# A hand-written planner gets new prices: TensorE's durations, a port that VectorE and GpSimd share, and the time at which an attention head's inputs land

## The chip, the cores and the metric

One core of one Trainium2 chip. The metric is the device time of one launch in microseconds (us), lower is better. Engines: TensorE (PE; its weight loads are listed as PEld), VectorE (DVE), ScalarE (ACT), GpSimd (POOL) and SyncE (SP), which here issues nearly all DMAs.

## The reference

One layer of a hybrid encoder, for two request groups that share the weights: 16 meta tokens and 512 prompt rows, and 64 new rows of a running stream, so 592 rows of 2048 columns, all fp32.

```
h = rms_norm(x, pre_gain)
g_q, g_k, g_v, g_z, g_r, s_q, s_k, s_v, s_z, m_gla, m_sb = split(h @ w_in)      # 2048 x 11280
o_gla = gated linear attention(g_q, g_k, g_v, decay from g_r)                  # 4 heads, 128 x 256 state
o_sb  = stick-breaking attention(s_q, s_k, s_v)                                # 8 heads, 1024 past keys for the 64 rows
y_gla = (rms_norm(o_gla) * silu(g_z)) @ w_up_gla;  y_sb = (o_sb * silu(s_z)) @ w_up_sb
y = x + rms_norm((sigmoid(m_gla) * y_gla + sigmoid(m_sb) * y_sb) @ w_o, post_gain)
```

Also returned are the new keys, the new values and the final states of the linear attention.

## The kernel before, in words

The four large products (`w_in`, `w_up_gla`, `w_up_sb`, `w_o`) are made on TensorE in three passes: each fp32 operand is split into a high part and a remainder (names ending in `h`/`hi` and `l`/`lo`), and high x high, high x low and low x high are added up in PSUM. The products with `w_in` and all but the first pair of `w_o` use a seven-product Strassen form on 2x2 blocks. The work is cut into *units* of 12 matmuls of 128x128 weights by 288 (or 296) columns. For each unit ScalarE rounds the weights (`convert`, tile `whi`), VectorE forms the remainder (`remain`, tile `wlo`), and at most four units are converted ahead of TensorE. The Strassen sums of weights (`combine`, `raw<-raw`) and the sums of results (`queue`: tiles `u`, `out`) run on VectorE; in one pair of columns the last product, S4 (reads block `h2`), may start only when the product S2 has been taken out of its bank by VectorE's `u` additions. A pair has the products W11, W22, S3, S1, S2, W12, S4, which read the blocks h0, h6, h5, h3, h4, h1, h2.

The attention runs in the background of these units, as generators: `decays` and four `gla_head`s one after the other (with `gla_side`, which takes half of a head's levels), then the eight heads of the stick-breaking attention, each as five chains (`sb_chain`, two of them interleaved). After the last unit of `w_in` come the two up-projections, then `w_o` and the final norm.

The order of the instructions on every engine is fixed when the program is built. A `Plan` keeps for each engine the time at which it is free and for each tile the time at which it is ready, and prices every instruction with `cost`. `Plan.run` holds one stream for each of the generators (`convert`, `remain`, `combine`, `multiply`, `queue`, ..., the background); again and again it takes the stream whose `due` time is the earliest, lets it issue its next instructions, and `note` moves the times on:

```
def due(self, e):
    return max(e["ready"] + e["slack"], self.free.get(e["eng"], 0.0)) - self.lead.get(e["name"], 0.0)
```

`e["ready"]` of a stream is `plan.last` at its last yield; `note` sets `plan.last` to the end of each priced instruction. In `w_in` the leads are 0.4 for `remain` and `combine`, 0 for `queue`, -0.1 for `multiply`; background streams have a slack of 0.4. So the prices decide nothing but the order in which instructions stand on the engines. On the chip every engine goes through its own list in that order and waits where an operand is not there.

The change touches `Plan.__init__`, a new `Plan.shared`, `Plan.cost`, `Plan.note`, and the start of `gla_head`. There a head takes `st["at"]`, the planned landing of its inputs k, cs and q (`gla_fetch`: five DMAs on SP and three small memsets on POOL), a tile `sc` is cleared by POOL, the flag ("load", hh) lets `gla_side` begin (its first instructions are VectorE's `x<-cs` subtractions), and `gla_diag` issues TensorE's products `b<-q,k`. The inputs of head 0 are fetched when the head begins; those of heads 1 to 3 while the head before is being normed, if g_q and g_k are stored by then.

Of the kernel before, what the change touches and what calls it, by code (L numbers as in the profile page):

```python
# [9 lines left out]
F32 = mybir.dt.float32  # L10
# [68 lines left out]
class Plan:  # L79


    def __init__(self):
        self.free, self.ready, self.used, self.last, self.streams = {}, {}, {}, 0.0, []
        self.base, self.now = {}, 0.0
        self.quartered, self.psum, self.lead, self.by = set(), set(), {}, {}

    def names(self, x):
# [8 lines left out]
    def at(self, x):  # L96
        return max(self.ready.get(y, 0.0) for y in self.names(x))

    def cost(self, eng, name, out, ins, summed):
        n = 1  # L100
        for x in out.shape[1:]:
            n *= x
        psum = any(x.tensor.name in self.psum for x in ins)
        if eng == "pe":
            dt = ins[0].dtype
            if dt == BF16:
                return 0.107
            if name == "transpose":
                return 0.053 if n < 64 else 0.11
            return max(0.214, n * 1.67e-3) if dt == F32 else max(0.11, n * 0.42e-3) + 0.003  # L110
        if eng == "act":
            return (0.055 if psum else 0.095) + (0.09 if summed or len(ins) > 1 else 0.0) + n * 0.83e-3
        if eng == "dve":
            if name == "tensor_scalar" and not psum:
                return 0.07 + n * 0.52e-3
            return 0.07 + n * (6.3e-3 if name == "reciprocal" else 1.04e-3)
        if name == "memset":
            return 0.04 + n * 0.83e-3
        return 0.15 + n * (3.5e-3 if name == "tensor_scalar" else 2.1e-3)

    def note(self, eng, name, args, kw):
        aps = [x for x in list(args) + list(kw.values()) if isinstance(x, bass.AP)]
        out = kw["out"] if "out" in kw else args[0]
        ins = [x for x in aps if x is not out]
        names = [y for x in ins for y in self.names(x)]
        outs = self.names(out)
        made = outs[1:] or outs
        if "dma" in name:
            size = 4.0
            for x in out.shape:  # L130
                size *= x
            start = max([self.now, self.free.get(eng, 0.0)] + [self.ready.get(x, 0.0) for x in names] + [self.base.get(outs[0], 0.0)])
            self.free[eng] = start + 0.5
            self.free["dma"] = max(self.free.get("dma", 0.0), start + 1.9) + size / 350e3
            end = self.free["dma"] + 1.8
            for x in made:
                self.ready[x] = max(self.ready.get(x, 0.0), end)
            for x in names:
                self.used[x] = max(self.used.get(x, 0.0), end)
            return  # L140
        start = self.free.get(eng, 0.0)
        for x in names + outs:
            by = self.by.get(x)
            if eng != "pe" or by != "pe":
                start = max(start, self.ready.get(x, 0.0) + LATENCY.get((by, eng), 0.1))
        end = start + self.cost(eng, name, out, ins, "accum_out" in kw)
        self.free[eng] = end
        for x in names + outs:
            self.used[x] = max(self.used.get(x, 0.0), end)
        for x in made:  # L150
            self.ready[x] = self.base[x] = end
            self.by[x] = eng
        self.last = end
# [54 lines left out]
def hybrid_step_kernel(ctx: ExitStack, tc: tile.TileContext, a, o):  # L208
    nc = tc.nc
    plan = Plan()  # L210
    sync, act, dve, pool, pe = (
        Engine(plan, key, e)
        for key, e in (("sp", nc.sync), ("act", nc.scalar), ("dve", nc.vector), ("pool", nc.gpsimd), ("pe", nc.tensor))
    )
# [513 lines left out]
    st = Region("st", "right")  # L728
# [480 lines left out]
    def gla_head(hh):  # L1209
# [3 lines left out]
            gla_fetch(hh)  # L1213
        st = gst[hh]
        k, cs, q = st["k"], st["cs"], st["q"]
        plan.last = max(plan.last, st["at"])
        sc = st["sc"] = r.tile([P, GC], F32, "sc")
        pool.memset(sc, 0.0)
        yield
        gdone.add(("load", hh))  # L1220
        yield from gla_diag(hh)
# [13 lines left out]
        end = r.tile([P, 6], F32, "end")  # L1235
# [5 lines left out]
        t = plan.last  # L1241
# [6 lines left out]
        t = plan.last  # L1248
        tokens(v0, scratch["gv", 2 * hh])
        at = plan.last  # L1250
# [10 lines left out]
        for j in range(2):  # L1261
            s = r.tile([P, 5, P], F32, "s")
            s5 = r.tile([P, P], F32, "s5")
            t = plan.last
# [41 lines left out]
            t = plan.last  # L1306
# [8 lines left out]
        t = plan.last  # L1315
# [3 lines left out]
        at = plan.last  # L1319
# [27 lines left out]
        for j in range(2):  # L1347
            yield "dve"
            x = o_t[j][:, :TO]
            dve.scalar_tensor_tensor(x, x, ggain[:, hh, j : j + 1], rs, op0=ALU.mult, op1=ALU.mult)  # L1350
        plan.last = max(plan.last, at)
        for j in range(2):
            yield "dve"
            x = o_t[j][:, :TO]
# [367 lines left out]
    def background():  # L1722
# [10 lines left out]
        for hh in range(GH):  # L1733
            yield from gla_head(hh)
# [239 lines left out]
```

## Time and profile before

| | |
|---|---|
| time, median of 3 runs | 1744.12 us (1739.87 to 1744.42) |
| time of the profiled execution | 1741.68 us |
| its span, first to last instruction | 1739.9 us |
| TensorE busy | 1670.2 us, 96% of the span |
| VectorE busy | 1250.6 us, 72% |
| ScalarE busy | 853.8 us, 49% |
| GpSimd busy | 182.2 us, 10% |
| mean granted TensorE clock | 0.986 of full speed |

The profiled execution lies inside the three runs, and 1.8 us of its time lie outside the span. All engine instructions go through one helper, so they carry the line L197, and groups are told apart by the names of their tiles: `wlo<-raw,whi` is the remainder, `b` is a PSUM bank. Consecutive instructions of one engine overlap a little in the trace (the end of one lies behind the start of the next), so a run of n instructions in a row tells the price of one better than the duration of a single one.

### The profile page before, as it was taken

Reading aid. Unit: us, or ns where it says so; the run is one execution under the profiler, and the core shown is the slowest. Engines: PE = TensorE matmul, PEld = TensorE weight load, DVE = VectorE, ACT = ScalarE, POOL = GpSimd, SP = SyncE. Lnnn points to the kernel's source line nnn. Section 1 sums busy time; section 2 is a strip of 40 time slices with the busy share of each in tenths; the row PEclk is TensorE's granted clock in tenths of the full one; section 3 lists DMA queues with packets and bytes.
Section 4 is the critical chain, followed back from the end, with each engine's and each line's share of the span. In section 5 each row is a group of like instructions: output and inputs, shape, how many; then the busy total and the mean of one; then the engine's idle time right before and its main releaser. Section 6 shows DMA issues by size and latency. Waiting matters only on the chain.

```text
span 1739.9 us, 31534 instructions
## 1 busy us (share of the span) xinstructions
PE 1670.2 (96%) x12089; PEld 1610.1 (93%) x12089; DVE 1250.6 (72%) x2081; ACT 853.8 (49%) x1759; POOL 182.2 (10%) x293
## 2 busy tenths in 40 slices
PE   4998999899999999999999999999999999999997
PEld 2798999889999998999999999999999999999996
DVE  5877878887987886886677667666766435687777
ACT  5554444344454353455565555555544323355554
POOL 2100220120130021021020011111000000000000
PEclk9999999999999999999999999999999999999998
DMA  7144234344444424455445544554447444423336
GB/s 189 37 140 131 77 107 139 101 116 123 122 117 128 132 60 119 126 163 159 133 137 152 148 140 117 158 158 126 128 138 218 143 142 124 122 79 103 104 80 218
DMA packets 323904, 224.14 MB, mean 129 GB/s; under 512 B 17436, under 2 KB 293432, under 8 KB 322584
## 3 DMA queue, kind: packets, MB, share of 16 engines
q1 hardware_dynamic: 323016, 219.49, 44.3%
q10 hardware_dynamic: 736, 2.62, 0.4%
q8 instruction: 95, 1.56, 0.4%
q14 instruction: 57, 0.47, 0.1%
HBM read 179.17 MB, written 42.90 MB: 128 GB/s over the span
## 4 chain that ended last, share of the span: by engine, by line
PE 89%; DVE 5%; DMA 2%; ACT 1%; issue 1%; POOL 1%; SPq 0%; DVEq 0%; ACTq 0%; POOLq 0%
PE b L197 89%; DVE wlo L197 2%; DVE raw L197 1%; DMA xt<-in_x_sample 1%; ACT whi L197 0%; DVE u L197 0%; DVE t L197 0%; DMA q<-d_gq 0%; POOL h5l L197 0%; DMA xt<-in_x_prompt 0%; DVE x L197 0%; POOL L L197 0%; DVE out L197 0%; SPq L197 0%; DMA raw<-in_w_in 0%
## 5 line engine op out<-in xcount | busy, mean ns | idle before, releaser
L197 ACT CAST whi<-raw 128x512 fp32r<-128x512 f32 x786 | 482.0, 620 | 627.6 <-PE b L197 516.2
L197 DVE TENSOR_TENSOR wlo<-raw,whi 128x512 fp32r<-128x512 f32 x786 | 552.6, 713 | 303.9 <-ACT whi L197 293.7
L197 DVE TENSOR_TENSOR raw<-raw 128x1024 f32<-128x1024 f32 (+1 forms) x232 | 259.5, 1121 | 6.0
L197 PE MATMUL b<-m,whi 128*128 128x288 f32 x912 | 183.5, 296 | 0.0
L197 PEld LDWEIGHTS b<-m,whi 128*128 128x128 f32 x912 | 146.1, 188 | 0.0
L197 PE MATMUL b<-h0h,whi 128*128 128x288 f32 (+1 forms) x480 | 134.3, 304 | 1.3 <-ACT whi L197 1.3
L197 PE MATMUL b<-m,wlo 128*128 128x288 f32 x456 | 134.2, 294 | 0.0
L197 PE MATMUL b<-h6h,whi 128*128 128x288 f32 (+1 forms) x480 | 133.8, 303 | 0.0
L197 PE MATMUL b<-h6l,whi 128*128 128x288 f32 (+1 forms) x480 | 131.5, 298 | 1.9 <-DVE h6l L197 1.8
L197 PE MATMUL b<-h4h,whi 128*128 128x288 f32 (+1 forms) x480 | 133.0, 302 | 0.0
L197 PE MATMUL b<-h1h,whi 128*128 128x288 f32 (+1 forms) x480 | 132.1, 300 | 0.0
L197 PE MATMUL b<-h0l,whi 128*128 128x288 f32 (+1 forms) x480 | 131.5, 299 | 0.0
L197 PE MATMUL b<-h4l,whi 128*128 128x288 f32 (+1 forms) x480 | 130.4, 296 | 0.0
L197 PE MATMUL b<-h1l,whi 128*128 128x288 f32 (+1 forms) x480 | 130.3, 296 | 0.0
L197 PE MATMUL b<-h0h,wlo 128*128 128x288 f32 (+1 forms) x416 | 124.4, 299 | 1.5 <-DVE wlo L197 1.5
L197 PE MATMUL b<-h4h,wlo 128*128 128x288 f32 (+1 forms) x416 | 123.2, 296 | 1.6 <-DVE wlo L197 1.6
L197 PE MATMUL b<-h1h,wlo 128*128 128x288 f32 (+1 forms) x416 | 123.3, 296 | 0.8 <-DVE wlo L197 0.8
L197 PE MATMUL b<-h6h,wlo 128*128 128x288 f32 (+1 forms) x416 | 123.7, 297 | 0.0
L197 PE MATMUL b<-h2h,whi 128*128 128x288 f32 (+1 forms) x352 | 112.5, 319 | 10.7 <-DVE u L197 10.7
L197 PE MATMUL b<-h2h,wlo 128*128 128x288 f32 (+1 forms) x352 | 107.5, 305 | 1.0 <-DVE wlo L197 1.0
L197 PE MATMUL b<-h5h,whi 128*128 128x288 f32 (+1 forms) x352 | 108.5, 308 | 0.0
L197 PE MATMUL b<-h3h,whi 128*128 128x288 f32 (+1 forms) x352 | 107.9, 307 | 0.0
(263 smaller groups left out, 4084.8 us busy)
## 6 DMA issues: line engine op xcount, KB each, us to landing
raw<-in_w_in SPq DMA_DIRECT2D x176, 512.0 KB, 4.5
raw<-in_w_o SPq DMA_DIRECT2D x32, 512.0 KB, 4.0
raw<-in_w_up_gla SPq DMA_DIRECT2D x16, 512.0 KB, 5.3
raw<-in_w_up_sb SPq DMA_DIRECT2D x16, 512.0 KB, 4.7
d_mg<-out SPq DMA_DIRECT2D x16, 288.0 KB, 2.2
d_ms<-out SPq DMA_DIRECT2D x16, 288.0 KB, 2.1
gate<-d_mg SPq DMA_DIRECT2D x16, 288.0 KB, 5.4
gate<-d_ms SPq DMA_DIRECT2D x16, 288.0 KB, 5.5
```

The costliest lines, as they stand in the source:

```text
L197: return real(*args, **kw)
```

## The change

Four edits to the planner and one to the start of a head; no instruction is added, removed or resized.

```diff
@@ Plan.__init__
+        self.port = {"pool": [], "dve": []}
...
+    def shared(self, out, ins):
+        n = [x for x in ins if x.tensor.name not in self.psum and x.shape[1:] == out.shape[1:]]
+        return len(n) > 1
@@ Plan.cost
             if dt == BF16:
-                return 0.107
+                return 0.056
             if name == "transpose":
-                return 0.053 if n < 64 else 0.11
-            return max(0.214, n * 1.67e-3) if dt == F32 else max(0.11, n * 0.42e-3) + 0.003
+                return 0.11
+            return max(0.224, n * 1.67e-3 + 4e-3) if dt == F32 else max(0.112, n * 0.4167e-3 + 0.0125)
...
+            if name == "scalar_tensor_tensor" and len(ins) > 2:
+                return 0.125 + n * 1.04e-3
@@ Plan.note
-        end = start + self.cost(eng, name, out, ins, "accum_out" in kw)
+        took = self.cost(eng, name, out, ins, "accum_out" in kw)
+        if name != "memset" and (eng == "pool" or eng == "dve" and self.shared(out, ins)):
+            for t0, t1 in sorted(self.port["pool" if eng == "dve" else "dve"]):
+                if t0 < start + took and t1 > start:
+                    start = t1
+            self.port[eng] = self.port[eng][-23:] + [(start, start + took)]
+        end = start + took
@@ gla_head
-        plan.last = max(plan.last, st["at"])
+        t = plan.last
         sc = st["sc"] = r.tile([P, GC], F32, "sc")
         pool.memset(sc, 0.0)
+        plan.last = max(t, st["at"])
         yield
```

- TensorE: a matmul of a unit (288 columns) goes from 0.1240 to 0.1325 us, one of 296 columns from 0.1273 to 0.1358; fp32 matmuls rise by 0.004 to 0.01 us, short transposes from 0.053 to 0.11, and bfloat16 ones fall from 0.107 to 0.056.
- VectorE: a `scalar_tensor_tensor` with three tensor inputs costs 0.055 us more.
- The port: a GpSimd instruction other than a memset, and a VectorE instruction with two inputs in SBUF, are moved behind every instruction of the other engine, among its last 24 of that kind, that they would overlap.
- The landing: `note` set `plan.last` to the end of the memset of `sc`, over the landing time taken just before; now the landing time is taken behind the memset, together with the stream's own time `t`.

## Rows read from the trace of the kernel before

**Rows 1.** The page, part 1: busy us (share of the span) xinstructions.

```profile
PE 1670.2 (96%) x12089; PEld 1610.1 (93%) x12089; DVE 1250.6 (72%) x2081; ACT 853.8 (49%) x1759; POOL 182.2 (10%) x293
```

**Rows 2.** Busy us (x instructions) by stage: PE, PEld, DVE, ACT, POOL, clock, DMA.

```profile
150.00:680.00 530.00, 500.69 (x3640) 489.94 (x3639) 429.49 (x712) 246.31 (x485) 88.82 (x113) 0.97 0.40 114
680.00:1266.00 586.00, 584.75 (x4267) 561.23 (x4266) 399.26 (x617) 320.28 (x632) 67.54 (x144) 1.00 0.49 139
1350.00:1700.00 350.00, 350.00 (x2639) 350.00 (x2639) 223.56 (x392) 150.66 (x338) 0.00 (x0) 1.00 0.39 110
```

**Rows 3.** PE's waits, 150 to 680 us: total, times, longest.

```profile
PE b L197 <- DVE u L197: 10.7, 3, 4.2
PE b L197 <- DVE cs L197: 5.8, 4, 2.7
PE b L197 <- DMA q<-d_gq: 5.5, 1, 5.5
PE b L197 <- DVE wlo L197: 3.4, 5, 1.6
PE b L197 <- DMA x<-d_gv: 2.7, 2, 1.4
PE b L197 <- DVE x L197: 1.3, 3, 0.6
```

**Rows 4.** PE's waits, 680 to 1700 us.

```profile
PE b L197 <- POOL L L197: 1.2, 3, 0.4
PE b L197 <- DVE h6l L197: 1.0, 1, 1.0
```

**Rows 5.** Busy us in the six stretches of halved clock, 150 to 680.

```profile
167.50:174.20 6.70, 3.55 (x16) 3.58 (x17) 2.72 (x6) 1.71 (x3) 1.19 (x1) 0.50 0.33 112
...
sum 33.30, PE 24.36 PEld 24.45 DVE 21.11 ACT 8.92 POOL 8.06; mean PE 4.06 PEld 4.08 DVE 3.52 ACT 1.49 POOL 1.34
```

**Rows 6.** Timeline of PE, 163 to 176: start, us, instruction, [idle before <-releaser].

```profile
164.81 0.29 PE L197 MATMUL b<-h2h,wlo 128*128 128x288 f32 x1
170.65 2.05 PE L197 MATMUL b<-q,k 128*128 128x128 f32 x8 [5.54 <-DMA q<-d_gq]
```

**Rows 7.** Timeline of SP and of DVE, 154 to 182.

```profile
165.42 0.84 SPq L197 DMA_DIRECT2D q<-d_gq  x2
...
164.87 2.48 DVE L197 TENSOR_TENSOR raw<-raw 128x1024 f32<-128x1024 f32 x2
169.97 0.90 DVE L197 TENSOR_TENSOR x<-cs 128x320 f32<-128x320 f32 x2 [2.62 <-DMA cs<-d_cs]
170.78 0.69 DVE L197 TENSOR_TENSOR wlo<-raw,whi 128x512 fp32r<-128x512 f32 x1
```

**Rows 8.** Timeline of DVE and of POOL, 362 to 380.

```profile
365.01 4.83 DVE L197 TENSOR_TENSOR wlo<-raw,whi 128x512 fp32r<-128x512 f32 x3 [0.27 <-ACT whi L197]
376.27 2.49 DVE L197 TENSOR_TENSOR wlo<-raw,whi 128x512 fp32r<-128x512 f32 x4
...
365.30 2.03 POOL L197 TENSOR_TENSOR x<-x,k 128x640 f32<-128x640 f32 x1
367.28 2.01 POOL L197 TENSOR_TENSOR q<-q,x 128x640 f32<-128x640 f32 x1
```

**Rows 9.** Timeline of DVE and of POOL, 300 to 322, where head 1 begins.

```profile
306.23 0.75 DVE L197 TENSOR_TENSOR x<-x,s 128x576 f32<-128x576 f32 x1
310.72 0.89 DVE L197 TENSOR_TENSOR x<-cs 128x320 f32<-128x320 f32 x2 [3.74 <-DMA d_og<-x]
...
317.00 2.48 DVE L197 TENSOR_TENSOR raw<-raw 128x1024 f32<-128x1024 f32 x2
319.40 0.95 DVE L197 TENSOR_TENSOR u<-u,b 128x296 f32<-128x296 f32 x2
...
303.87 0.63 POOL L197 MEMSET sc<- 128x640 f32 x1 [14.00 <-PE b L197]
```

**Rows 10.** DVE's waits, 150 to 680 us: total, times, longest.

```profile
DVE x L197 <- DMA d_og<-x: 7.4, 3, 3.7
```

## The prediction

> **What bounds the kernel now.** I read the page's busy shares first [rows 1]: TensorE is busy for 1670 of 1740 us, so the kernel is bound by TensorE, and no edit here removes a matmul. Only the time in which it stands still or runs slowly can be won. To see where that is I took the busy times by stage [rows 2]. From 1350 to 1700 us (up-projections and `w_o`) it is busy in all of the 350 us, and 2639 matmuls start in them, one every 0.1326 us. From 680 to 1266 us (stick-breaking attention) 1.3 us are missing. From 150 to 680 us (linear attention) 29.3 us are missing of 530, with VectorE busy in 81% of it. The waits of TensorE give the causes: in that stage `u`, `cs`, `wlo` and `x`, all made by VectorE (21.2 us together), then the inputs of a head (5.5) and of its values (2.7) [rows 3]; later, two small ones [rows 4]. The rest of its idle time is the start, before 75 us, and the last 24 us.
>
> Idle time is not all. The stage's granted clock is 0.97 [rows 2], and the stretches of low clock are six, each beside one of the longer waits: there the clock is 0.50, the lower of its two levels (1.2 of 2.4 GHz), and TensorE is busy for 24.4 of 33.3 us [rows 5]. Work at half speed loses half of its time, 12.2 us. So the whole stake in the stage is 29.4 + 12.2 = 41.6 us, 2.4% of the time.
>
> **The change part by part.** The edits change prices in the planner, so they act only through the order.
>
> *The landing.* TensorE finishes the first half of S4 at 165.10 and then stands for 5.54 us in front of `b<-q,k` of head 0, until q lands [rows 6]; the other half of S4, 12 matmuls, stands behind it in the list. VectorE waits 2.62 us in front of `x<-cs` in the same way [rows 7]. The planner put these there because the memset's end overwrote the landing time. After the change the stream of head 0 comes back only at the landing that the planner works out, 1.9 us + 0.97 MB at its 350 GB/s (2.8) + 1.8 = 6.5 us from the first issue, and up to 3 us more where weights are still under way. The trace has 170.65 - 165.42 = 5.2 us from the issue of q to its first reader [rows 6, 7], and four issues of some 0.4 ahead of it, 6.9: the planner is near enough, or late, which costs nothing while units are left. What moves is the whole start of the head: its diagonal products on TensorE, VectorE's two masked copies and the first `x<-cs` of both streams, ScalarE's exponentials and GpSimd's products. Its five DMAs stay where they are in SP's list; the stores behind them follow later or earlier with VectorE. Gain: 5.54 us of wait, and in the half-clock stretch right behind it 3.55 us of work that loses 1.78 [rows 5]: 7.3. What is late next: the next pair's first `wlo`. VectorE is at `raw<-raw` until 167.35, then needs 0.69 [rows 7], so `wlo` is there at 168.04, while TensorE ends S4 at 165.10 + 12 x 0.1326 = 166.69. Up to 1.35 us of a new wait remain. I take 6.6 (bounds 6.0 and 7.3).
>
> For heads 1 to 3 the inputs were fetched early, and the landing is past. But the stream's time changes too: it was the memset's end, 303.87 + 0.63 = 304.50 for head 1, and is now the end of the norm's last product, 306.98 [rows 9], 2.5 us later. There VectorE stands 3.74 us in front of `x<-cs`, because a store still reads the tile that it overwrites; the `wlo` and `raw` behind it are late, and the `u` that S4 needs comes at 319.40. A later start may let some of those pass. All three head changes have this wait, 7.4 us in sum [rows 10]. I count this edit inside the term of the two edits below.
>
> *TensorE's prices.* A unit was priced 12 x 0.1240 = 1.488 us, and is now 1.590; the trace has 12 x 0.1326 = 1.591 [rows 2]. The planner thought TensorE 6.5% faster against the other engines than it is, and so expected operands to be wanted earlier, and VectorE to be more behind, than is true. The fp32, transpose and bfloat16 prices and the `scalar_tensor_tensor` one concern background instructions alone. I put them at nothing: the units cover them, as the full stages show [rows 2]; without that cover they would be worth as much as the small waits, 1.2 us [rows 4].
>
> *The port.* Three `wlo` took 4.83 us while GpSimd ran two products of 2 us; four `wlo` without GpSimd took 2.49, 0.62 each [rows 8]. So VectorE stood 2.97 us for GpSimd's sake, and the planner did not know. Each head makes one such pair, before its `cs` copies, and `cs` is what TensorE waits for four times, 2.7 us at the longest [rows 3]. The edit does not remove the blocking; it lets the planner put what needs a late VectorE later on TensorE, with units ahead of it.
>
> The Trainium skill (SBUF — State Buffer, section Who interferes with whom) says that whichever of the two starts first holds the shared port for its whole instruction, and the other waits for that one instruction. Rows 8 agree. The planner goes further: it sends an instruction behind each recorded one that it would overlap until a gap of its own length comes, so by that rule it now believes GpSimd later than it is, and half of the next term's gain would go: 1735.
>
> What the two edits are worth: the stake left is 29.4 - 5.5 = 23.9 us of waits and 12.2 - 1.8 = 10.4 of clock, 34.3 together. The bounds are 0 and 34.3. The part after GpSimd's pairs (`cs` 5.8, `wlo` 3.4 [rows 3], and some 3 of clock, an estimate: a quarter of the 12.2) is 12 us; I take half of it, 6. Of the `u` waits, which hang on the store that no edit touches, and their clock, some 18 us, I take 1. That is 7.
>
> *What a new order costs.* The stages that are full now need not stay so. Bounds: 0, and 18 us (rival 3). I take 3, nearer the rows, which show 2.2 us of such waits in 1020 us [rows 4].
>
> Sum, against the profiled execution's own 1741.7 (2.4 under the median of the runs): 1741.7 - 6.6 - 7 + 3 = **1731**. Own range: 1724 to 1738.
>
> **The rivals.**
> 1. *The true prices clear most of the stage.* All waits but the store's and the values' are from a planner that did not know how late VectorE was. Then 60% of the 34.3 goes too: 1741.7 - 7.3 - 20.6 = 1714. For it: the waits are few and long (three of `u` make 10.7 us), each with a half-clock stretch behind it. Against: `remain` and `combine` keep their lead of 0.4 over `queue`, so a late VectorE still makes `wlo` and `raw` ahead of `u`, as happened where `u` came behind two `raw` [rows 9].
> 2. *It only shifts.* Head 0 starts later, VectorE's bunch of `raw`, `wlo` and `u` meets the first levels in another place, and another wait of 4 us with its clock takes the place of the one removed. The time stays at 1741. For it: VectorE has only 100 us left in the stage [rows 2].
> 3. *The cheap TensorE was a cushion* (slower). With units priced 6.5% short, TensorE came later to each background product than planned, and its operands were there. Stick-breaking attention has 8 heads x 5 chains x 3 such arrivals (scores, tails, values) = 120, of which 3 wait now, 1.2 us [rows 4]. With the true price, what else is priced short shows. If each of 120 waits 0.15 us, that is 18 us: 1741.7 - 6.6 + 18 = 1753. For it: nothing else in the planner covers such errors but the slack of 0.4. Against: TensorE is always behind there, so a product is placed behind a queue of units. It decides from 12 us of waits between 680 and 1266 on.
>
> **How the numbers follow.** Forecast 0.4, rival 1 0.2, rival 2 0.2, rival 3 0.2. A measurement of this kernel tells about 0.3% from no change, 5.2 us around 1744.1: under 1738.9 is faster, over 1749.3 slower. The forecast and rival 1 are faster, 0.6; rival 2 same, 0.2; rival 3 slower, 0.2. The range reaches just past the middle of rival 1's and to that of rival 3: 1712 to 1753.
>
> **What the profile after would show.** Right: no wait of TensorE on `q<-d_gq` over 1 us and no half-clock stretch near 167; `cs` waits under 3 us in sum; the stage's missing time near 18 us; 680 to 1700 still full. Wrong: `u` waits of more than 11 us in sum (rival 2), waits on `L`, `t` or `h` of many short pieces (rival 3), or a stage with under 8 us missing (rival 1). It would also be wrong if the last 24 us, whose order the new prices shuffle too and where every instruction is on the path, grew by more than 3 us.

## The result and the profile after

The change makes the kernel slower by half a per cent. Over six runs each on the same chip the median goes from 1741.83 us (1737.65 to 1744.42) to 1751.47 us (1749.03 to 1755.23); the ratio is 1.0056, with an interval of 1.0039 to 1.0074, outside the 0.3% that a measurement of this kernel can tell. The forecast of 1731 us had the wrong sign. The time lies outside the forecast's own range (1724 to 1738) and inside the wide one (1712 to 1753) only because that one was drawn out to rival 3's time. The profiled execution took 1752.33 us with a span of 1750.5.

The busy times by stage, in the columns of [rows 2], with one more line for the hand-over from `w_in` to the up-projections:

```profile
150.00:680.00 530.00, 502.54 (x3635) 489.63 (x3634) 430.08 (x704) 250.47 (x490) 86.12 (x111) 0.97 0.40 114
680.00:1266.00 586.00, 583.15 (x4261) 561.29 (x4261) 404.15 (x627) 315.86 (x628) 68.56 (x147) 1.00 0.50 140
1266.00:1350.00 84.00, 80.67 (x567) 78.34 (x566) 52.99 (x78) 39.12 (x63) 3.19 (x4) 0.96 0.57 169
1350.00:1700.00 350.00, 350.00 (x2639) 350.00 (x2638) 221.44 (x386) 149.71 (x337) 0.00 (x0) 1.00 0.40 114
```

The linear attention's stage has not been cleared. It misses 27.5 us of 530, where it missed 29.3 [rows 2], and its clock is still 0.97. TensorE's waits in it (150 to 680 us; total, times, longest) are others than before:

```profile
PE b L211 <- DVE x L211: 10.2, 5, 4.5
PE b L211 <- ACT whi L211: 5.2, 3, 2.1
PE b L211 <- DMA x<-d_gv: 4.6, 3, 3.4
PE b L211 <- DVE u L211: 3.8, 1, 3.8
PE b L211 <- DVE wlo L211: 2.4, 5, 0.7
...
PE b L211 <- DMA q<-d_gq: 0.2, 1, 0.2
```

Against [rows 3] the waits on `cs` (5.8) and `q` (5.5) are gone and those on `u` fall from 10.7 to 3.8; but `x`, the decayed queries and keys of the heads, grows from 1.3 to 10.2, `whi` comes in with 5.2 and the values grow from 2.7 to 4.6. Each wait of 2 us or more still lies beside a stretch of half clock. In place of the six stretches of [rows 5] there are five, and they are as long in sum (length, then the busy times):

```profile
sum 33.60, PE 24.73 PEld 23.66 DVE 27.84 ACT 12.73 POOL 8.62; mean PE 4.95 PEld 4.73 DVE 5.57 ACT 2.55 POOL 1.72
```

The timeline of TensorE shows the landing's repair and what follows it. The first product of head 0 stands 38 us later than in [rows 6] and waits 0.20 us instead of 5.54; the first long wait on a level product behind it is 4.45 us:

```profile
208.99 1.13 PE L211 MATMUL b<-q,k 128*128 128x128 f32 x8 [0.20 <-DMA q<-d_gq]
...
247.29 1.09 PE L211 MATMUL b<-x 128*128 128x64 f32 x4 [4.45 <-DVE x L211]
```

The later place is not the landing's doing. In e11 (below), which lacks the landing edit, the product starts at 208.6; in e4, which lacks the port edit, at 175.9.

A new loss lies at the hand-over. The last block of the linear attention's result is loaded (`stage`), and ScalarE waits for it before it makes `h6l`, for which TensorE then waits 2.34 us; the granted clock of 1266 to 1350 falls from 1.00 to 0.96. TensorE's and ScalarE's timelines after, and then ScalarE's same instruction in a second execution of the kernel before, where it waits for nothing:

```profile
1336.64 0.40 PE L211 MATMUL b<-h6l,whi 128*128 128x288 f32 x1 [2.34 <-ACT h6l L211]
```

```profile
1335.43 1.15 ACT L211 CAST h6l<-stage 128x1152 fp32r<-128x1152 f32 x1 [2.21 <-DMA stage<-d_og]
```

```profile
1331.17 1.16 ACT L197 CAST h6l<-stage 128x1152 fp32r<-128x1152 f32 x1
```

Compared unit by unit, the profile of after is 1.9 us behind that of before at the first unit, 4.65 us behind at the 7200th matmul of units, and 9.53 us behind from the 7680th on. The 1.9 is chance: the second execution of the kernel before starts as late (below). So some 2.7 us were lost by the end of the stick-breaking attention, 4.9 at the hand-over, and 1 in the last stage, where TensorE's wait on `diag` grew from 1.2 to 2.2 us.

Most of this loss is work at half clock and not idle time. TensorE idles for 74.3 us after and for 73.5 in that second execution of before, but its busy time for the same 12089 matmuls grows from 1669.0 to 1676.2 us. Two stretches of half clock stand where the kernel before has none, one behind waits on `whi` and `wlo` near 786 (0.9 and 1.1 us), one at the hand-over. Their windows after, and the same windows in the second execution of before; about half as many matmuls run in the same time:

```profile
787.80:791.10 3.30, 3.30 (x16) 3.30 (x15) 1.94 (x6) 0.62 (x1) 0.00 (x0) 0.50 0.91 252
1337.30:1344.10 6.80, 6.07 (x25) 6.07 (x26) 2.23 (x4) 0.85 (x2) 0.00 (x0) 0.50 0.84 272
```

```profile
787.80:791.10 3.30, 3.30 (x27) 3.30 (x26) 1.79 (x4) 2.12 (x6) 0.00 (x0) 1.00 0.40 115
1337.30:1344.10 6.80, 6.80 (x53) 6.80 (x52) 2.21 (x4) 2.88 (x4) 0.00 (x0) 1.00 0.42 156
```

### The profile page after: what moved, and what is told of

It reads as the page before. It is cut to its first block, busy times and chain, and to the rows that moved or that the text cites. A ratio compares the mean times of both kernels' runs of the same rounds, so it can differ in the third digit from the quotient of the medians.

```text
span 1750.5 us, 31506 instructions
## 1 busy us (share of the span) xinstructions
PE 1676.2 (96%) x12089; PEld 1614.2 (92%) x12089; DVE 1252.8 (72%) x2081; ACT 854.1 (49%) x1759; POOL 180.9 (10%) x293
## 4 chain that ended last, share of the span: by engine, by line
PE 90%; DVE 4%; DMA 2%; issue 2%; ACT 1%; POOL 1%; SPq 0%; DVEq 0%; ACTq 0%; POOLq 0%
PE b L211 90%; DVE wlo L211 1%; DMA xt<-in_x_sample 1%; DMA stage<-d_og 0%; DVE x L211 0%; DMA x<-d_gv 0%; DVE raw L211 0%; ACT whi L211 0%; SPq L211 0%; POOL h5l L211 0%; DMA xt<-in_x_prompt 0%; DVE out L211 0%; DVE t L211 0%; POOL x L211 0%; DMA q<-d_gq 0%
## 5 line engine op out<-in xcount | busy, mean ns | idle before, releaser
L211 DVE TENSOR_TENSOR wlo<-raw,whi 128x512 fp32r<-128x512 f32 x786 | 546.9, 706 | 308.0 <-ACT whi L211 291.9
L211 PE MATMUL b<-h1h,whi 128*128 128x288 f32 (+1 forms) x480 | 136.5, 309 | 0.0
L211 PE MATMUL b<-h3h,wlo 128*128 128x288 f32 (+1 forms) x352 | 106.1, 301 | 2.0 <-DVE wlo L211 2.0
```

The lines of the kernel that those rows point to most:

```text
L211: return real(*args, **kw)
```

## The experiments

All ratios are to the kernel before on the same chip, with a 95% interval; "us" is what that ratio adds to or takes from 1741.8. Idle is the span less TensorE's busy time, "clock" is what the mean granted clock took off the span ((1 - clock) x span). These two are of one execution each; the second execution of before has 73.5 and 26.1.

| run | ratio | us | idle | clock |
|---|---|---|---|---|
| before | 1 | 0 | 69.7 | 24.4 |
| the change | 1.0056 [1.0039, 1.0074] | +9.8 | 74.3 | 33.3 |
| e1 landing alone | 1.0010 [0.9999, 1.0021] | +1.7 | 74.7 | 20.9 |
| e2 TensorE's prices alone | 0.9932 [0.9915, 0.9949] | -11.8 | 62.5 | 13.8 |
| e3 port alone | 1.0256 [1.0240, 1.0273] | +44.6 | 103.5 | 42.9 |
| e4 all but the port | 0.9955 [0.9941, 0.9970] | -7.8 | 67.1 | 17.3 |
| e11 all but the landing | 1.0101 [1.0082, 1.0119] | +17.6 | 84.6 | 31.7 |
| e5 port, VectorE's side alone | 1.0251 [1.0235, 1.0266] | +43.7 | 99.1 | 48.1 |
| e9 port, until head 0 | 1.0171 [1.0152, 1.0189] | +29.8 | 87.8 | 44.3 |
| e10 port, from head 0 on | 1.0234 [1.0212, 1.0256] | +40.8 | 98.9 | 46.4 |
| e6 port alone, first come | 1.0075 [1.0059, 1.0090] | +13.1 | 80.6 | 33.3 |
| e7 the change, first come | 0.9912 [0.9897, 0.9927] | -15.3 | 61.9 | 15.5 |
| e16 e7 without the landing | 0.9953 [0.9936, 0.9971] | -8.2 | 64.1 | 22.5 |
| e17 e7, `queue` led by 0.4 | 1.0017 [1.0005, 1.0029] | +3.0 | 70.7 | 22.6 |
| e8 before, nudged up | 1.0094 [1.0074, 1.0113] | +16.4 | 83.8 | 31.6 |
| e15 before, nudged down | 1.0062 [1.0042, 1.0082] | +10.8 | 78.1 | 28.0 |
| e14 e2, nudged | 1.0023 [1.0005, 1.0040] | +4.0 | 70.7 | 20.9 |
| e12 the change, nudged | 1.0094 [1.0063, 1.0125] | +16.4 | 77.8 | 37.0 |
| e13 e7, nudged | 0.9916 [0.9883, 0.9948] | -14.6 | 62.6 | 15.5 |

Idle time at half clock counts in both columns. If it is counted once, with half of the time that TensorE is busy at half clock in place of the last column, the rest of the span is 1649 to 1654 us in all twenty traces, while the spans go from 1724.5 to 1786.6. So what differs between these kernels is time in which TensorE stands, and the half clock that goes with it.

**The kernel before once more (e0),** one execution, no edit.

> The kernel before once more, for a second profile on another chip or at another time. It tells how much of two places is chance of the execution: the first units start at 60.9 us before and 62.8 after though the instructions ahead are the same, and at the change from the input products to the up-projections the load of the fourth operand lands 5.5 us after its issue before and 7.6 after. Chance theory: these two places vary here by 1 to 3 us with the same instructions. Order theory: both are as in the first profile of before, within 0.5 us.

It took 1744.31 us, with a span of 1742.5 against 1739.9. The first unit's first matmul starts at 62.68 us here and at 62.79 in the profile after, against 60.87 in the first profile of before; TensorE's timeline of this run, and then of after:

```profile
62.68 0.41 PE L197 MATMUL b<-h0h,whi 128*128 128x296 f32 x1 [1.32 <-ACT whi L197]
```

```profile
62.79 0.41 PE L211 MATMUL b<-h0h,whi 128*128 128x296 f32 x1 [1.33 <-ACT whi L211]
```

So differences of 2 us at the start are chance; against this execution the span of after is 8.0 us longer.

**Each part alone (e1 to e3) and the change less one part (e4, e11).** e1 keeps only the edit in `gla_head`, e2 only TensorE's prices in `cost`, e3 only `port`, `shared` and the loop in `note`. e4 takes the loop out of the change, e11 the edit in `gla_head`:

```diff
 # e4
-        took = self.cost(...)
-        if name != "memset" and (eng == "pool" or eng == "dve" and self.shared(out, ins)):
-            ...
-        end = start + took
+        end = start + self.cost(...)
 # e11
-        t = plan.last
+        plan.last = max(plan.last, st["at"])
...
-        plan.last = max(t, st["at"])
```

> The edit of the landing alone, on the kernel before. Landing theory (the step of the prediction): the wait of TensorE on head 0's q, 5.5 us, and its half-clock stretch go and little else moves, so 5 to 7 us faster than before, a ratio near 0.996 to 0.997. Reshuffle theory (any new order deals the waits of the linear-attention stage anew): the q wait goes, but other waits of about its size come in, so within 4 us of before either way.

> TensorE's new prices alone. Cushion theory (rival 3): slower by 8 to 12 us, with more than 12 us of TensorE waits between 680 and 1266 us. Port theory (the port edit is what costs): within 4 us of before or faster, the background ending some 50 units earlier. Reshuffle theory: within 6 us either way, with no waits on the stick-breaking tiles.

> The port edit alone. Port theory: slower by 8 to 12 us, as the whole change, because in the planner the background's VectorE steps come later, head 0 begins about 21 units later and the waits are dealt anew for the worse. Cushion theory: no slower than before, since TensorE stays cheap. Reshuffle theory: within 6 us either way.

> The whole change without its port edit: TensorE's prices, the price of scalar_tensor_tensor and the landing. Port theory: the port edit is the only one that costs, so this is as fast as TensorE's prices alone, 1726 to 1735 us, 0.5 to 0.9% under before. Reshuffle theory: the prices' gain was one lucky order, and with the head 0 shifted it comes out within 6 us of before, 1737 to 1750.

> The whole change without the landing. If the landing does in this order what it was meant to do, a wait on q of 3 to 10 us is back and the time is 3 to 10 us over the whole change, 1754 to 1762. Reshuffle theory: it may as well be faster than the whole change, by up to 10 us.

The landing alone changes nothing that can be told: 1.0010, as the reshuffle theory had it. The wait on `q` is gone and `u` falls from 10.7 to 6.2, but GpSimd's `x` is new and the values' wait grows from 2.7 to 5.7. Of TensorE's waits of 150 to 860 us:

```profile
PE b L197 <- POOL x L197: 7.3, 2, 4.2
PE b L197 <- DVE u L197: 6.2, 3, 2.6
PE b L197 <- DMA x<-d_gv: 5.7, 3, 2.5
```

TensorE's prices alone gain 11.8 us. The linear attention's stage misses 18.3 us there and runs at 0.99, and the stick-breaking stage has one group of waits, 3.2 us in four:

```profile
150.00:680.00 530.00, 511.74 (x3759) 499.38 (x3758) 437.97 (x733) 255.14 (x502) 88.92 (x115) 0.99 0.42 119
```

```profile
PE b L197 <- POOL L L197: 3.2, 4, 1.6
```

The port alone costs 44.6 us. Within the change it costs too: e4, without it, is at -7.8, and the change at +9.8. TensorE's waits in e3, 150 to 840 us:

```profile
PE b L209 <- DVE x L209: 23.3, 6, 7.2
PE b L209 <- DMA q<-d_gq: 9.6, 1, 9.6
PE b L209 <- ACT whi L209: 8.3, 7, 3.4
PE b L209 <- POOL x L209: 5.3, 3, 2.5
```

The longest on `x`, in the timelines of TensorE, VectorE and GpSimd in turn:

```profile
399.37 2.36 PE L209 MATMUL b<-x 128*128 128x64 f32 x10 [7.23 <-DVE x L209]
```

```profile
386.34 1.21 DVE L209 TENSOR_TENSOR raw<-raw 128x1024 f32<-128x1024 f32 x1
...
393.36 0.45 DVE L209 SCALAR_TENSOR_TENSOR e<-out 128x288 f32<-128x288 f32 x1
393.73 1.39 DVE L209 COPY_PREDICATED sc<-lmask,b 128x320 f32<-128x320 int32 x2
394.92 0.91 DVE L209 TENSOR_TENSOR x<-cs 128x320 f32<-128x320 f32 x2
...
397.58 1.24 DVE L209 SCALAR_TENSOR_TENSOR e<-out 128x288 f32<-128x288 f32 x1 [1.38 <-POOL out L209]
398.74 0.48 DVE L209 TENSOR_TENSOR x<-x,q 128x320 f32<-128x320 f32 x1
```

```profile
396.75 0.79 POOL L209 TENSOR_TENSOR out<-out,e 128x288 f32<-128x288 f32 x1 [10.69 <-ACT e L209]
397.51 1.00 POOL L209 TENSOR_TENSOR x<-x,k 128x320 f32<-128x320 f32 x1
```

TensorE stands for `x` until its last product ends at 399.2. The `x<-cs` for it stood in VectorE's list behind weight sums (`raw`), and that last product behind two other instructions and a wait for GpSimd, which had itself idled 10.69 us. What holds VectorE there is mostly its place in the lists; the port's part is some 0.8 us (an estimate: `e<-out` takes 1.24 us beside GpSimd's product and 0.45 without it).

**Which side, and when (e5, e9, e10).** e5 sends only VectorE behind GpSimd; e9 applies the rule until head 0 begins, e10 from there on.

```diff
 # e5, on e3
-            for t0, t1 in sorted(self.port["pool" if eng == "dve" else "dve"]):
+            for t0, t1 in sorted(self.port["pool"]) if eng == "dve" else []:
 # e9, on e3 (e10: self.begun); gla_head sets plan.begun = True
-        if name != "memset" and (eng == "pool" or ...):
+        if name != "memset" and not self.begun and (eng == "pool" or ...):
```

> The port edit alone, and of it only one side: VectorE is sent behind the recorded instructions of GpSimd, GpSimd is not sent behind VectorE's. Future-claim theory (VectorE is sent behind GpSimd instructions that are planned to start after it, which makes it late in the plan and starves the background's steps): slower by 25 to 50 us, as with both sides; head 0's first product stands 21 units later. Long-queue theory (it is GpSimd that is sent too far back, past several VectorE instructions, and with it all that reads its products): within 10 us of before.

> The port edit alone, and only until head 0 begins; from there on the planner knows no port, as before. Late-start theory (the 44 us come from the decays and head 0 standing 20 units later): slower by 30 us or more. Bunching theory (they come from the heads' levels, whose VectorE and GpSimd steps the rule reorders): within 12 us of before.

> The port edit alone, and only from head 0's beginning on; decays and head 0 stand where they stand before. Late-start theory: within 12 us of before. Bunching theory: slower by 30 us or more, with TensorE's waits on x as in the port edit alone.

VectorE's side alone costs the whole 44 us; GpSimd's side was not run by itself. Both stretches cost, 30 and 41 us, so neither theory of the two holds alone, and together (e3) they cost little more than the later one alone; the late start of head 0 is not all of it.

**First come (e6, e7, e16, e17).** An instruction now waits only for one of the other engine that is running at its own start, not for those planned to begin after it. e6 is this rule alone, e7 the whole change with it, e16 is e7 without the edit in `gla_head`, e17 is e7 with another lead.

```diff
-            for t0, t1 in sorted(self.port["pool" if eng == "dve" else "dve"]):
-                if t0 < start + took and t1 > start:
-                    start = t1
+            start = max([start] + [t1 for t0, t1 in self.port["pool" if eng == "dve" else "dve"] if t0 <= start < t1])
 # e17 besides, in LEADS
-'queue': 0,
+'queue': 0.4,
```

> The port edit alone with the rule that whichever starts first holds: an instruction waits only for the one that runs on the other engine when it would start, not for one planned to start later, and not for a row of them. Future-claim theory: the 44 us are gone, and the time is within 8 us of before. Rival (any late VectorE in the plan costs, while TensorE is priced short): still 20 us slower or more.

> The whole change with that rule in place of its own. Port theory: about as TensorE's prices alone, 1725 to 1737 us, so 15 to 25 us under the change as it is. Reshuffle theory: 1740 to 1752, no better than the change by more than 8 us.

> The first-come version without the landing. Landing theory: TensorE waits 3 to 10 us on head 0's q again, and the time is 4 to 10 us over the first-come version, 1731 to 1738. Reshuffle theory: within 4 us of it or under it, the q wait taken back by fewer others.

> The first-come version with a lead of 0.4 for queue in the input products, as remain and combine have. If u comes late because wlo and raw go ahead of it whenever VectorE is behind, TensorE's waits on u go and the time falls by 3 to 8 us, to 1720 to 1725. Rival: the lead makes wlo and raw late instead, TensorE waits on wlo, and the time rises by 3 us or more.

e7, with 1727.6 us and 0.9912 of before, is the fastest kernel of this study together with its nudge e13 (0.9916, below). Its stage from 150 to 680, and TensorE's waits of 150 to 860:

```profile
150.00:680.00 530.00, 512.72 (x3765) 500.59 (x3763) 444.93 (x734) 254.32 (x500) 91.64 (x117) 0.99 0.42 118
```

```profile
PE b L209 <- DVE x L209: 9.5, 8, 5.5
PE b L209 <- DMA x<-d_gv: 3.2, 2, 3.1
PE b L209 <- DVE wlo L209: 2.4, 1, 2.4
...
PE b L209 <- DVE u L209: 0.7, 1, 0.7
```

It misses 17.3 us where the change misses 27.5, at a clock of 0.99 instead of 0.97. Over the whole span the two are 24.6 us apart: idle time falls by 12.4, and TensorE's busy time for the same matmuls by 12.2 (1676.2 to 1664.0). e6 alone is still at +13.1, between what its two theories said and between the nudges of before (below), so the milder rule gains nothing by itself. e17 was to show whether `u` starves behind `wlo` and `raw`. Its time rose by 18.3 us over e7, but not on `wlo` (1.2 us); the `u` waits were small in e7 and are small here, while `x` grew, so it doesn't tell:

```profile
PE b L209 <- DVE x L209: 12.6, 4, 6.1
PE b L209 <- POOL x L209: 5.9, 3, 5.0
PE b L209 <- DVE u L209: 0.9, 2, 0.5
```

**What any new order costs (e8, e12 to e15).** One figure of a unit's price is moved by less than half a per cent, and nothing else.

```diff
 # e8 (e15: 0.4185e-3), on before
-max(0.11, n * 0.42e-3) + 0.003
+max(0.11, n * 0.4215e-3) + 0.003
 # e12 on the change, e14 on e2 (e13 on e7: 0.4182e-3)
-max(0.112, n * 0.4167e-3 + 0.0125)
+max(0.112, n * 0.4152e-3 + 0.0125)
```

> The kernel before with a meaningless change of TensorE's price, a unit's matmul at 0.1244 us for 0.1240 (0.35%). It alone moves head 0 back by 20 units, as the port edit does. Reshuffle theory: such a nudge moves the time by 5 us or more, either way, so results of this size need no cause in what an edit means. Meaning theory (only a wrong or a right price moves the time): within 4 us of before.

> The whole change with TensorE's price lowered by 0.35% (0.1321 us for a unit's matmul). Family theory (the full port rule costs some 20 us under true prices): 1744 to 1762. Reshuffle theory: it may fall anywhere from 1727 to 1765, so below 1740 in one case of two.

> The first-come version of the change with TensorE's price raised by 0.35% (0.1329 us). Family theory: 1722 to 1737. Reshuffle theory: anywhere from 1727 to 1765, over 1740 in one case of two.

> TensorE's new prices alone, lowered by 0.35%. Family theory: 1722 to 1740. Reshuffle theory: anywhere from 1727 to 1765, over 1740 in one case of two.

> The kernel before with TensorE's price nudged the other way, 0.1235 us for 0.1240. Its first half of the order is that of before. Luck theory (the order of before is a good one among those of the cheap price): slower, 1745 to 1762. Meaning theory: within 4 us of before.

Both nudges of before make it slower, by 16.4 and 10.8 us; nudging costs e2 15.8 us, the change 6.6 and e7 0.7. The waits of e8, 150 to 860 us, are of the same kinds as everywhere:

```profile
PE b L197 <- DVE x L197: 9.6, 5, 4.2
PE b L197 <- POOL x L197: 9.0, 2, 4.7
PE b L197 <- DMA x<-d_gv: 8.9, 4, 5.2
PE b L197 <- DMA q<-d_gq: 5.8, 1, 5.8
```

The family theory's range for e2's nudge ended at 1740, and e14 is above it; those for e12 and e13 held, and so did the luck theory's for e15. So a single order says little below 0.9%, and the parts are to be judged by groups of orders. With the full port rule and true prices there are three: +9.8, +16.4, +17.6. With the first-come rule four: -15.3, -14.6, -8.2 and, with a lead changed, +3.0. The pairs that differ in the rule alone, the change and e7, and e11 and e16, lie 25 and 26 us apart. That is beyond every nudge, and the groups don't meet. With true prices and no port rule at all there are three, e2, e4 and e14: -11.8, -7.8, +4.0. They lie among those of the first-come rule, so it is not shown to be better than none.

## Why the prediction was wrong, step by step

**What bounds the kernel** held. Idle time and work at half clock account for the differences to within some 5 us, and the stake of 41.6 us in the linear attention's stage was real: e2 and e7 took out a good part of it.

**The landing** (6.6 gained) was right in its mechanism and unsure in its size. The wait on `q` went from 5.5 to 0.2 us, and there is no half-clock stretch near 167. Where the edit is missing the wait is there: 3.4 us in e2, 5.8 in e8, 8.4 in e11, 2.9 in e16; with it the most is 1.4 (e12). The same edit is worth 7.8 us within the change (e11 against it), 7.1 with the first-come rule (e16 against e7), and nothing alone (e1); e4, which adds it and the `scalar_tensor_tensor` price to e2, is 4.0 slower than e2. As the nudges move as much, the times don't show its worth; only the wait's end is shown. That another wait with its clock takes the place of one removed was rival 2, and it is what the stage shows in e1 and in the change, whose stage lost a total as large as before.

**TensorE's prices and the port** (7 gained) is the step that failed, and in it the port. The two edits were sized as one term. TensorE's prices alone gave 11.8 us, of the forecast sign, but a nudge took that away (e14, 4.0 slower than before). The port was taken as part of a gain, and it costs: 44.6 us alone, and 17.6 between e4 and the change. The prediction did see the fault, that the planner's loop sends an instruction behind each recorded one that it would overlap while on the chip it waits for one, but it named the wrong engine and size: "GpSimd later than it is", 4 us, which its sum left out. It is VectorE's side that costs (e5, 43.7 of the 44.6), and the rule's price within the change is 25 us (e7 against the change). The Trainium skill (SBUF — State Buffer, section Who interferes with whom) states that a VectorE instruction with two inputs in SBUF contends with a GpSimd instruction that reads SBUF, and that whichever is issued first has the shared port for its whole instruction while the other is blocked. No run here times the port by itself, but [rows 8] fit it: taken singly, the three `wlo` end at 365.90, 367.87 and 369.84, each 0.55 us behind one GpSimd instruction (365.35, 367.32, 369.29).

**`u` and `cs`.** The `cs` waits are gone, as forecast, but the `u` waits were given 1 us of their 18 because the store behind them was untouched; they fell to 3.8 in the change and to 0.7 in e7. VectorE still waits for that store, 4.7 us where it was 7.4 [rows 10]:

```profile
DVE x L211 <- DMA d_og<-x: 4.7, 3, 1.7
```

**The cost of a new order** (3, bounds 0 and 18) was mis-sized: orders that differ by a nudge of no meaning lie 0.7 to 16 us apart. The kernel before is the fastest of the three orders with its prices, the other two being 11 and 16 us behind. The value of 3 was read from stages that are full under one order, which says nothing of the next.

**Rival 3** had the nearest time (1753), not the cause. It decides from 12 us of waits between 680 and 1266; there are 2.8 us in the change, 3.2 in e2, and true TensorE prices are no loss. What was not foreseen is the hand-over, 4.9 us of the change's profile; but fifteen of the other runs, e7 among them, wait there for ScalarE's `h6l` too, for 1.2 to 2.2 us. Neither execution of before does, nor e15. Why the load is late in the others was not shown. **Rival 1** (1714) came out in no run; without the port's rule the change is at 1734.9 (e4) and with the first-come one at 1727.6 (e7), both inside the forecast's own range.

**What stays open.** Why a VectorE that the planner believes late ends in real waits on `x` was argued (streams with a lead of 0.4 are let in ahead of background ones) and not shown; e17 was to tell and didn't. It was not separated either whether the port edit costs by waiting for work that has not begun or by waiting for several instructions in a row; the first-come rule takes away both. The landing's worth and that of the `scalar_tensor_tensor` price were not separated from chance; the latter was run only with other parts.

## What to carry to other kernels

Beware of a planner's price for a shared resource that reserves it ahead for every recorded instruction: it makes the planner reorder for delays that the trace does not show, and here that cost 17.6 us more than leaving the blocking out (the change against e4). A price by who starts first was 25 us better, though not better than none. Where an order is written from prices, move one price by a fraction of a per cent before believing a gain or a loss: here that alone is worth up to 0.9%, so compare groups of orders, and judge a repaired wait in the trace, not in the total. A tuned order can be a lucky draw from its group, as the one of before is among its three; count on losing that luck with any edit.

## What the runs showed of the hardware

Two executions of one program start their first unit 1.8 us apart (60.87 and 62.68 us). The load of `stage` ahead of `h6l` took 8.4 us from the start of its issue (1326.99) to its reader in the change's profile, while in the first profile of before its reader, held by nothing, started 6.3 us after it (1322.34 to 1328.59). The granted clock's losses (last column of the table) rise with the idle time, though not in step: 13.8 to 15.5 us where TensorE idled some 62 us, 43 to 48 where it idled about 100, but 20.9 and 33.3 in two runs where it idled 74 to 75. VectorE's `wlo` takes 0.62 us without GpSimd and 2.05 us when it comes up behind a GpSimd product, of which each took 2.0 us beside it (singly, in the stretch of [rows 8]).
